# Issuing one tensor's early loads from a second engine's queue in a row-wise Poisson loss

## Chip, cores, metric

One core of one Trainium2 chip. The time is device microseconds of a whole execution; the lower the better. The profile's span (first to last instruction) is 1.34 us shorter than that time, since it leaves out what the device does around the program.

All times below are of fast runs: no kernel's runs differ by more than 0.6%, and the granted clock is 1.0 in every one. Ratios are the mean time of one kernel's fast runs over that of the other's in the same rounds, so they are not quite the ratio of the medians that are quoted.

## The reference

```
log_input, target: 1024 x 4096 float32
loss = exp(log_input) - target * log_input
out  = mean(loss, axis=-1)            # 1024 float32
```

Both inputs are 16.8 MB, the result 4 KB. Per element there is one exponential (ScalarE) and one product with a running sum (VectorE).

## The kernel before

Each of the 128 partitions holds 8 whole rows. Below, "x" is log_input and "t" is target. The loads come in this order: x rows 0-3, t rows 0-3, x rows 4-5, t rows 4-5, x row 6, t row 6, then row 7 in seven small pieces. Rows 0-3 live in x_big and t_big, rows 4-5 in x_mid and t_mid. Row 6 reuses the place of row 0 and row 7 that of row 3, so those loads wait for the work on these rows.

```python
TAIL = [("x", 98), ("t", 50), ("t", 48), ("x", 24), ("t", 18), ("x", 6), ("t", 12)]
# ... cut
    loads = []
    for first, rows in ((0, 4), (4, 2), (6, 1)):
        loads += [("x", first * d, rows * d), ("t", first * d, rows * d)]
# ... cut: TAIL appended, buffers, one semaphore per load
    early = []
    for i, (what, lo, w) in enumerate(loads):
        if what == "x" and lo in (6 * d, 7 * d):
            free = 1 if lo == 6 * d else 4
            nc.sync.wait_ge(exp_done, free)
            nc.sync.wait_ge(prod_done, free)
        src = x_v if what == "x" else t_v
        dma = nc.sync.dma_start(out=place(what, lo, w), in_=src[:, lo : lo + w])
        dma.then_inc(landed[i] if i < len(loads) - 1 else last_ready, 16)
        if lo < 6 * d:
            early.append(dma.ins)
    before_first_barrier(nc, early)     # moves them ahead of the program's first barrier
# ... cut
    # ScalarE, per row: exp with a row sum, waiting for landed[x]; from row 2 on a small
    # "join" ahead of it that adds up row - 2, waiting for that row's product
    # VectorE, per row: product with a row sum, waiting for landed[x] and landed[t]
```

## Time and profile before

| | before |
|---|---|
| median time | 84.02 us (83.93 to 84.27, 3 runs) |
| span in the profile | 82.5 us |
| VectorE, ScalarE busy | 35.6 us, 33.2 us |
| packets on 16 DMA engines | 95.8% of the span, one queue |
| first product on VectorE | 41.12 us |
| first exponential on ScalarE | 21.80 us |

Read the table from the DMA row up. The transfer engines are full; both compute engines are idle for more than half the span, and most of that idle time is at the front, waiting for the first rows. In all lines of the profile DVE is VectorE, ACT is ScalarE and POOL is GpSimd; SPq and ACTq are the queues in which SyncE and ScalarE issue, q1 and q10 the DMA queues that these fill; L129 is a line of the kernel. A packet is one piece of data that an engine moves in one go, here one partition's share of a load. A barrier is a point at which all engines wait for each other; the program has three before the kernel's own work. Where ScalarE waited before the change (the list of waits: engine and line, what it waited for, us in total, times, longest):

```profile
ACT e_dump L155 <- DMA x_big<-in_log_input_dram: 23.6, 3, 17.6
ACT join_dump L141 <- DVE parts L175: 20.3, 6, 16.3
```

ScalarE got rows 0-3 of x early, did two exponentials, and then stood 16.3 us before its first join, until VectorE had a product for it.

### The profile page before, as it was taken

What the parts mean: (1) busy time and instruction counts of PE and PEld (TensorE: products, weight loads), DVE (VectorE), ACT (ScalarE), POOL (GpSimd) and SP (SyncE); (2) the same over time, 40 slices, a digit from 0 to 9 for tenths busy, and PEclk for the clock granted to TensorE, in tenths of its full rate; (3) what the DMA queues carried; (4) which work ended last, traced back from release to release, by engine and by line L of the source; (5) the groups of instructions that cost most, each with busy time, mean ns of one, the idle gap of its engine ahead of it and who ended that gap; (6) DMA issues with size and microseconds to landing.
All of it is one profiled execution on the core that took longest, in us unless ns stands there. A gap on an engine that the chain in (4) does not pass through costs nothing.

```text
span 82.5 us, 131 instructions
## 1 busy us (share of the span) xinstructions
DVE 35.6 (43%) x22; ACT 33.2 (40%) x35; POOL 0.3 (0%) x5
## 2 busy tenths in 40 slices
DVE  0000000000000000000099999999369995993992
ACT  0500000000499920000000998979792496009460
POOL 0000000000000000000000000000000000000000
DMA  9289999929999992999599799799799999999960
GB/s 508 127 381 508 508 508 508 476 95 445 508 508 508 508 413 95 508 508 508 254 508 429 333 508 492 318 460 508 302 453 397 461 421 418 426 402 412 397 231 2
DMA packets 2016, 33.56 MB, mean 407 GB/s; under 512 B 352, under 2 KB 608, under 8 KB 1120
## 3 DMA queue, kind: packets, MB, share of 16 engines
q1 hardware_dynamic: 2016, 33.56, 95.8%
HBM read 33.55 MB, written 0.00 MB: 407 GB/s over the span
## 4 chain that ended last, share of the span: by engine, by line
DMA 72%; DVE 18%; issue 5%; SPq 3%; DVEq 0%
DMA t_big<-in_target_dram 49%; DMA x_big<-in_log_input_dram 23%; DVE t_big L175 17%; SPq L129 3%; DVE t_big L193 1%; DVE parts L175 0%; DVEq L192 0%; SPq L127 0%; DVE all_loss L193 0%
## 5 line engine op out<-in xcount | busy, mean ns | idle before, releaser
L175 DVE CUSTOM_DVE_ANT_0 t_big<-t_big,x_big 128x4096 f32<-128x4096 f32 (+3 forms) x8 | 26.2, 3308 | 43.5 <-DMA t_big<-in_target_dram 43.4
L155 ACT ACTIVATE e_dump<-x_big 128x4096 f32<-128x4096 f32 (+3 forms) x8 | 21.8, 2729 | 23.9 <-DMA x_big<-in_log_input_dram 23.6
L141 ACT ACTIVATE join_dump<-parts 128x2 f32<-128x2 f32 x7 | 1.4, 203 | 20.4 <-DVE parts L175 20.3
L175 DVE CUSTOM_DVE_ANT_0 t_mid<-t_mid,x_mid 128x4096 f32<-128x4096 f32 x2 | 8.8, 4424 | 2.0 <-DMA t_mid<-in_target_dram 2.0
L155 ACT ACTIVATE e_dump<-x_mid 128x4096 f32<-128x4096 f32 x2 | 7.1, 3568 | 0.0
L155 ACT ACT_TABLE_LOAD x1 | 1.3, 1283 | 2.9 <-PEq L48 2.9
L155 ACT ACTIVATION_READ_ACCUMULATOR e_dump<-x_big 128x1 f32 x8 | 1.5, 186 | 0.0
L141 ACT ACTIVATION_READ_ACCUMULATOR join_dump<-parts 128x1 f32 x7 | 1.3, 186 | 0.0
L175 DVE DVE_READ_ACCUMULATOR2_ANT parts<- 128x1 f32 x7 | 0.6, 84 | 0.0
L193 DVE CUSTOM_DVE_ANT_0 t_big<-t_big,x_big 128x390 f32<-128x390 f32 x1 | 0.6, 566 | 0.0
L155 ACT ACTIVATION_READ_ACCUMULATOR e_dump<-x_mid 128x1 f32 x2 | 0.4, 186 | 0.0
L175 DVE DVE_READ_ACCUMULATOR2_ANT t_big<- 128x1 f32 x3 | 0.2, 82 | 0.0
L136 POOL MEMSET x_big<- 128x6 f32 x1 | 0.1, 104 | 2.5 <-POOLq L48 2.5
L227 POOL MEMSET const-uint8-127<- 128x1 uint8 x1 | 0.1, 102 | 0.0
L227 POOL MEMSET const-bfloat16-1.0<- 128x1 bf16 x1 | 0.1, 101 | 0.0
L227 POOL MEMSET const-float32-0.0<- 128x1 f32 x1 | 0.1, 98 | 0.2 <-issue 0.2
L227 POOL MEMSET const-float32-1.0<- 128x1 f32 x1 | 0.1, 98 | 0.0
L193 DVE DVE_READ_ACCUMULATOR2_ANT all_loss<- 128x1 f32 x1 | 0.1, 82 | 0.0
## 6 DMA issues: line engine op xcount, KB each, us to landing
x_mid<-in_log_input_dram SPq DMA_DIRECT2D x1, 4096.0 KB, 49.9
t_mid<-in_target_dram SPq DMA_DIRECT2D x1, 4096.0 KB, 59.2
x_big<-in_log_input_dram SPq DMA_DIRECT2D x1, 2048.0 KB, 19.8
t_big<-in_target_dram SPq DMA_DIRECT2D x1, 2048.0 KB, 24.3
x_big<-in_log_input_dram SPq DMA_DIRECT2D x1, 1568.0 KB, 15.4
t_big<-in_target_dram SPq DMA_DIRECT2D x1, 800.0 KB, 17.0
t_big<-in_target_dram SPq DMA_DIRECT2D x1, 768.0 KB, 18.4
x_big<-in_log_input_dram SPq DMA_DIRECT2D x1, 384.0 KB, 18.9
```

The costliest lines, as they stand in the source:

```text
L129: dma = nc.sync.dma_start(out=place(what, lo, w), in_=src[:, lo : lo + w])
L136: nc.gpsimd.memset(big["x"][:, 4 * d : 4 * d + n_parts], -1.0).then_inc(ones_done, 1)
L141: nc.scalar.activation(out=join_dump[:, 2 * row : 2 * row + 2], in_=parts[:, 2 * row : 2 * row + 2], func=ACT_F.Copy, scale=inv_d, accum_o ...
L155: nc.scalar.activation(out=e_dump[:, col : col + w], in_=place("x", lo, w), func=ACT_F.Exp, bias=0.0, scale=1.0, accum_out=parts[:, 2 * ro ...
L175: nc.vector.tensor_tensor_reduce(out=place("t", lo, w), in0=place("t", lo, w), in1=place("x", lo, w), scale=-1.0, scalar=0.0, op0=ALU.mult ...
L193: nc.vector.tensor_tensor_reduce(out=place("t", lo, w + n_parts), in0=place("t", lo, w + n_parts), in1=place("x", lo, w + n_parts), scale= ...
L227: nc = _bacc.Bacc("TRN2", target_bir_lowering=False, num_devices=1)
```

## The change

All seven loads of t used to stand in SyncE's queue among those of x. The change lets ScalarE issue the two early loads of t (rows 0-3 and 4-5) in its own queue, also ahead of the first barrier, so that x and t set off together and SyncE has two issues less before the barrier.

```diff
-def before_first_barrier(nc, instructions):
+def before_first_barrier(nc, instructions, engine):
 ...
-        if i.engine == mybir.EngineType.SP and i.opcode == "Drain"
+        if i.engine == engine and i.opcode == "Drain"
 ...
-    early = []
+    early = {nc.sync: [], nc.scalar: []}
 ...
-        dma = nc.sync.dma_start(out=place(what, lo, w), in_=src[:, lo : lo + w])
+        issuer = nc.scalar if what == "t" and lo < 6 * d else nc.sync
+        dma = issuer.dma_start(out=place(what, lo, w), in_=src[:, lo : lo + w])
 ...
-            early.append(dma.ins)
-    before_first_barrier(nc, early)
+            early[issuer].append(dma.ins)
+    for issuer, instructions in early.items():
+        before_first_barrier(nc, instructions, issuer.engine)
```

On ScalarE two DMA instructions now stand first; on SyncE two are gone; no other engine's order changes.

## The prediction

> **What bounds the kernel now.** I read the page from the top, then the share of the DMA queue, then windows cut by hand, then the chain and the waits of the two compute engines.
>
> ```profile
> span 82.5 us, 131 instructions
> DVE 35.6 (43%) x22; ACT 33.2 (40%) x35; POOL 0.3 (0%) x5
> ...
> GB/s 508 127 381 508 508 508 508 476 95 445 508 508 508 508 413 95 508 508 508 254 508 429 333 508 492 318 460 508 302 453 397 461 421 418 426 402 412 397 231 2
> ...
> q1 hardware_dynamic: 2016, 33.56, 95.8%
> ```
>
> No compute engine is busy for half the span. The one queue's packets fill 95.8% of 16 DMA engines' 82.5 us, which is 79.0 us. The row of 40 slices seems to disagree: it has slices of 95 and 127 GB/s, which look like holes that a second queue might fill. They are not holes. The packets of the first loads are 64 KB each (a partition's four rows of 16 KB), and at 433 GB/s over 16 engines one takes 65,536 x 16 / 433 GB/s = 2.42 us, more than a slice of 82.5/40 = 2.06 us. A view that books a packet where it starts leaves some slices nearly empty. Windows cut where all engines have just begun a row of packets show this (us of the window, its length, busy us of DVE, ACT and POOL with counts, PE clock, DMA share, GB/s):
>
> ```profile
> 0.00:1.00 1.00, 0.00 (x0) 0.00 (x0) 0.20 (x4) 1.00 0.00 0
> 1.00:20.95 19.95, 0.00 (x0) 1.28 (x1) 0.10 (x1) 1.00 1.01 420
> 20.95:40.28 19.33, 0.00 (x0) 7.42 (x4) 0.00 (x0) 1.00 1.00 434
> 40.28:59.65 19.37, 17.47 (x8) 12.71 (x15) 0.00 (x0) 1.00 1.00 433
> 59.65:80.00 20.35, 17.11 (x11) 11.34 (x15) 0.00 (x0) 1.00 0.99 412
> 80.00:82.50 2.50, 1.04 (x4) 0.43 (x2) 0.00 (x0) 1.00 0.03 2
> ```
>
> The DMA share is 0.99 to 1.01 in every window from 1.0 to 80.0 us. So the span is 1.0 us before the first byte, 79.0 us of all 16 engines working without a break, and 2.5 us after the last byte (last product, result to HBM). The first window's 420 and the last one's 412 GB/s are the fill of the first packets and the small packets of the tail; in the middle the rate is flat at 433 to 434.
>
> The loads arrive in the order of the one queue, as the issue times below plus the page's times to landing say: x rows 0-3 at 21.8, t rows 0-3 at 0.4 + 40.7 = 41.1, x rows 4-5 at 0.9 + 49.9 = 50.8, t rows 4-5 at 1.4 + 59.2 = 60.6, then rows 6 and 7. The timeline shows what SyncE issues first and when VectorE may begin:
>
> ```profile
> 0.00 0.38 SPq L129 DMA_DIRECT2D x_big<-in_log_input_dram  x1
> ...
> 0.43 0.42 SPq L129 DMA_DIRECT2D t_big<-in_target_dram  x1
> 0.89 0.43 SPq L129 DMA_DIRECT2D x_mid<-in_log_input_dram  x1
> 1.37 0.50 SPq L129 DMA_DIRECT2D t_mid<-in_target_dram  x1
> ...
> 21.80 3.59 ACT L155 ACTIVATE e_dump<-x_big 128x4096 f32<-128x4096 f32 x1 [17.58 <-DMA x_big<-in_log_input_dram]
> ...
> 41.12 4.43 DVE L175 CUSTOM_DVE_ANT_0 t_big<-t_big,x_big 128x4096 f32<-128x4096 f32 x1 [41.12 <-DMA t_big<-in_target_dram]
> ...
> 60.55 4.43 DVE L175 CUSTOM_DVE_ANT_0 t_mid<-t_mid,x_mid 128x4096 f32<-128x4096 f32 x1 [1.96 <-DMA t_mid<-in_target_dram]
> ...
> 70.33 4.43 DVE L175 CUSTOM_DVE_ANT_0 t_big<-t_big,x_big 128x4096 f32<-128x4096 f32 x1 [1.00 <-DMA t_big<-in_target_dram]
> ...
> 76.05 1.83 DVE L175 CUSTOM_DVE_ANT_0 t_big<-t_big,x_big 128x1600 f32<-128x1600 f32 x1 [1.28 <-DMA t_big<-in_target_dram]
> ```
>
> After its first row VectorE waits for data three more times: 1.96, 1.00 and 1.28 us. Those 4.2 us are its slack.
>
> **What the Trainium skill says.** "DMA: Bandwidth & Descriptors", section "Issuing engines are not separate DMA queues": DMAs of SyncE and ScalarE run on the same 16 DMA engines, and issuing on several "will only save the time on the sequencer it takes to initiate the DMA". The trace of before, with one queue, cannot show two; what it shows is that four issues took 0.38 to 0.50 us each and all but the first lay under data already moving. The same page, "Where 436 GB/s comes from": the ports carry at most 435.2 GB/s. The trace's 433 to 434 is within half a per cent of it. The same page, "Queues, rings and completion order": each DMA engine goes round robin between queue rows, packet by packet. No run here shows that yet; the prediction rests on it for the order of landing.
>
> **The change part by part.**
>
> Bytes and packets: the same 33.56 MB in the same pieces on the same 16 engines. Nothing removed, nothing added: 0 us.
>
> Issue: t_big moves from second on SyncE (0.43 us) to first on ScalarE, t_mid from fourth (1.37 us) to second there. SyncE is through with its early issues about 0.9 us earlier (two issues of 0.42 and 0.50 us less), so the first barrier opens about that much earlier. What lies behind it is a table load of 1.28 us, after which ScalarE waited 17.6 us for data: 0 us on the path. The first load still leaves SyncE at 0, so the first byte still comes at 1.0 us. With two sequencers generating at once the 16 engines might get their first packet a little more evenly; I allow 0.2 us either way.
>
> Landing: x_big and t_big now share the engines. With equal packets taken in turn both are done when 16.8 MB are through, about 41 us, where t_big landed before. So t_big does not land earlier; x_big lands later, about 38.5 to 41 instead of 21.8. Likewise x_mid and t_mid both at about 59 to 60.5. Row 6 stands in SyncE's queue behind x_mid, and its landing (65.4 and 70.3) follows from bytes alone, as does that of row 7.
>
> VectorE needs both operands, so it starts at 41.1 as before and goes on as before.
>
> ScalarE loses its head start of two exponentials. Alone, an exponential takes 3.81 us from start to start (21.80 to 25.60 in the timeline); with a join in front I take 3.96 (from a join's 45.59 to its exponential's accumulator at 49.30 + 0.19, plus its gap). From 41.1: row 0, row 1 at 44.9, row 2 from 48.7, row 3 from 52.7 to 56.6, wait for x_mid at 60.5 at the latest, rows 4, 5, 6 end at about 64.3, 68.3, 72.3. The first piece of row 7 begins at 74.10 before, when its data land. Slack left: 1.8 us. ScalarE gives up idle time and nothing else.
>
> Buffer gates: row 6's load waits for row 0's exponential and product. The product still ends at 45.5 and the exponential at about 44.9, so the issue stays at 45.6, while SyncE's queue holds x_mid until about 59. Row 7's loads wait for four of each: products at 58.5, exponentials at 56.6, so 58.6 as before, with row 6's data (10 us of it) still ahead. Neither gate starves the engines.
>
> Tail: the loads after row 5 stay on SyncE in the same order and find the other queue empty from about 60 us; 2.5 us after the last byte, as before.
>
> Sum: 0 on bytes, 0 on landing of the later operand, 0 on tail, +-0.2 on the start. 84.02 becomes about 84.0.
>
> **The rivals.**
>
> Faster through bandwidth: two queues keep more reads in flight and lift the rate. For it: the low slices, and 420 GB/s in the first window. Against: the slices are an artefact, and the flat 433 lies at the port's limit. If even the first window ran at 434, its 8.38 MB would take 19.3 instead of 19.95 us: 0.6 us, 83.4, still within 2%.
>
> Slower through unequal shares: if SyncE's queue gets more than its turn, x_mid runs ahead of t_big and VectorE starts late. Its slack is 4.2 us, so t_big may land as late as 45.3 for nothing. For 2% (1.7 us) it must land at 47.0, when 45.4 us x 0.433 = 19.7 MB are through (taking 1.6 us for first byte and fill), of which t_big's 8.39 are 43%: SyncE would need 57% or more. At 60% t_big lands behind all of x_mid, near 50 us, and the time is near 84.0 + 4.7 = 88.7. Equal packet sizes speak against it.
>
> Slower through switching: if alternating between two tensors costs each 64 KB packet 1%, the first 60 us lengthen by 0.6 us: 84.6. Nothing in the trace of before speaks for or against.
>
> **Range and chances.** The centre is 84.0. Runs of before spread from 83.93 to 84.27. A gain of up to 0.5 us at the start and a loss of up to 0.7 from switching or a slightly skewed share give 83.5 to 84.7. Beyond 2% either way (82.3, 85.7) needs a fault in the main argument: above the port's rate I hold 0.01 likely, a share of 57% or more 0.04.
>
> **What would show it.** Right: about 1.00 DMA share from 1.0 to 80 us, now over two queues; ScalarE's first exponential at 38 to 41 us; VectorE's first product at about 41.1; waits of VectorE before rows 4 and 6 still positive; last byte at 80. Wrong: a first product after 45 us, or ScalarE busy without a wait before row 7 (then it has become the bound), or a middle rate away from 433 GB/s.

## The result, and the profile after

84.00 us median (83.94 to 84.18, 6 runs) against 84.02 (83.89 to 84.27, 6 runs): ratio 0.9997, 95% interval 0.9979 to 1.0015. The same.

The page of the changed kernel (span; then queue, packets, MB, share of 16 engines) has two queues whose shares add up to 95.8%, the share that the one queue had:

```profile
span 82.6 us, 131 instructions
...
q1 hardware_dynamic: 1728, 20.98, 60.6%
q10 hardware_dynamic: 288, 12.58, 35.2%
```

The windows of the changed kernel, cut again where a row of packets begins (columns as in the prediction):

```profile
0.00:0.99 0.99, 0.00 (x0) 0.00 (x0) 0.20 (x4) 1.00 0.00 0
0.99:20.90 19.91, 0.00 (x0) 1.28 (x1) 0.10 (x1) 1.00 1.01 421
20.90:40.22 19.32, 0.00 (x0) 0.00 (x0) 0.00 (x0) 1.00 1.00 434
40.22:59.58 19.36, 17.47 (x8) 15.51 (x14) 0.00 (x0) 1.00 1.00 433
59.58:80.01 20.43, 17.07 (x11) 15.94 (x18) 0.00 (x0) 1.00 0.99 411
```

DMA share and rate are those of before in every window: 421, 434, 433, 411 against 420, 434, 433, 412 GB/s. What moved is the ScalarE column: 7.42 us of work in the second window became 0.00, and the two windows after it took it up (15.51 and 15.94 instead of 12.71 and 11.34). The sum of its work is 33.2 us in both kernels.

The timeline of the changed kernel shows the same in single instructions:

```profile
0.00 0.38 SPq L131 DMA_DIRECT2D x_big<-in_log_input_dram  x1
0.12 0.37 ACTq L131 DMA_DIRECT2D t_big<-in_target_dram  x1
...
0.43 0.42 SPq L131 DMA_DIRECT2D x_mid<-in_log_input_dram  x1
0.52 0.45 ACTq L131 DMA_DIRECT2D t_mid<-in_target_dram  x1
...
2.05 1.28 ACT L158 ACT_TABLE_LOAD   x1 [2.05 <-PEq L49]
41.13 3.59 ACT L158 ACTIVATE e_dump<-x_big 128x4096 f32<-128x4096 f32 x1 [37.79 <-DMA x_big<-in_log_input_dram]
41.31 4.42 DVE L178 CUSTOM_DVE_ANT_0 t_big<-t_big,x_big 128x4096 f32<-128x4096 f32 x1 [41.31 <-DMA t_big<-in_target_dram]
...
60.56 3.59 ACT L158 ACTIVATE e_dump<-x_mid 128x4096 f32<-128x4096 f32 x1 [3.56 <-DMA x_mid<-in_log_input_dram]
60.75 4.43 DVE L178 CUSTOM_DVE_ANT_0 t_mid<-t_mid,x_mid 128x4096 f32<-128x4096 f32 x1 [1.97 <-DMA t_mid<-in_target_dram]
...
70.36 4.42 DVE L178 CUSTOM_DVE_ANT_0 t_big<-t_big,x_big 128x4096 f32<-128x4096 f32 x1 [0.83 <-DMA t_big<-in_target_dram]
...
74.14 2.79 ACT L158 ACTIVATE e_dump<-x_big 128x3136 f32<-128x3136 f32 x1 [1.50 <-DMA x_big<-in_log_input_dram]
...
76.07 1.82 DVE L178 CUSTOM_DVE_ANT_0 t_big<-t_big,x_big 128x1600 f32<-128x1600 f32 x1 [1.28 <-DMA t_big<-in_target_dram]
```

The first four lines are the change at work: all early issues are through after about 1 us. The table load begins at 2.05 instead of 2.93 us, which is the earlier barrier, 0.88 us, and then ScalarE stands idle for 37.79 us. Its first exponential starts 19.3 us later than before (41.13 for 21.80), yet before row 7 it still waits 1.50 us for data: it is behind and has caught up. VectorE's lines are those of before, 0.2 us later at the front and 0.02 us at the first piece of row 7.

### The profile page after: what moved, and what is told of

Its sections match the earlier page's. It is cut to its first block, busy times and chain, and to the rows that moved or that the text cites. A ratio compares the mean times of both kernels' runs of the same rounds, so it can differ in the third digit from the quotient of the medians.

```text
span 82.6 us, 131 instructions
## 1 busy us (share of the span) xinstructions
DVE 35.6 (43%) x22; ACT 33.2 (40%) x35; POOL 0.3 (0%) x5
## 4 chain that ended last, share of the span: by engine, by line
DMA 72%; DVE 22%; SPq 3%; issue 1%; DVEq 0%
DMA t_big<-in_target_dram 50%; DMA x_big<-in_log_input_dram 22%; DVE t_big L178 21%; SPq L131 3%; DVE t_big L196 1%; DVEq L195 0%; DVE parts L178 0%; SPq L128 0%; DVE all_loss L196 0%
## 5 line engine op out<-in xcount | busy, mean ns | idle before, releaser
L158 ACT ACTIVATE e_dump<-x_big 128x4096 f32<-128x4096 f32 (+3 forms) x8 | 21.8, 2727 | 41.1 <-DMA x_big<-in_log_input_dram 40.8
```

Source lines behind the costliest of these rows:

```text
L158: nc.scalar.activation(out=e_dump[:, col : col + w], in_=place("x", lo, w), func=ACT_F.Exp, bias=0.0, scale=1.0, accum_out=parts[:, 2 * ro ...
```

## The experiments

The theory: the 16 DMA engines are full, they serve the two queues in turn, piece by piece, and so the time is set by when the *later* operand of each row lands. The change leaves that as it is. The rivals: (a) the second queue brings a gain and a loss that cancel; (b) who issues, and in which order, never matters, only the bytes do; (c) VectorE is on the path as much as the transfers. The first four kernels ran on one chip (kernel before: 83.95 us median of 11 runs there), the last four on another (84.09, 11 runs). All gave correct results.

**e1: ScalarE's loads after the barriers.** The change with its early issue on ScalarE undone; SyncE keeps its own.

```diff
-        if lo < 6 * d:
+        if lo < 6 * d and issuer is nc.sync:
             early[issuer].append(dma.ins)
```

> Theory (the 16 DMA engines are full from 1.0 to 80 us and take packets from the two queues in turn, so who issues and when is hidden): the two target loads now leave ScalarE only after the first barriers, about 1.9 us later than in the changed kernel. The second row of packets starts at 4.0 us in the changed kernel, the new issue lands its first packet near 3 us, so nothing moves: 84.0 us, DMA share 1.00, first product at 41.3. Rival (a gain of the early issue on ScalarE and a loss of alternating cancel each other): without the early issue the loss stands alone, 84.3 us or more.

Measured: 84.08 us (83.91 to 84.12, 6 runs), ratio to before 1.0003 (0.9991 to 1.0016). Rival (a) said 84.3 or more and is out at this size. But one number of mine was wrong: the first product started at 42.55, not 41.3 (timeline).

```profile
1.91 0.37 ACTq L131 DMA_DIRECT2D t_big<-in_target_dram  x1
...
42.55 4.42 DVE L178 CUSTOM_DVE_ANT_0 t_big<-t_big,x_big 128x4096 f32<-128x4096 f32 x1 [42.55 <-DMA t_big<-in_target_dram]
```

By the trace's packet records t's first packet began at 6.5 us, after two of x's and not after one, so x stayed a packet ahead. VectorE took up the 1.2 us out of its waits (1.35 before row 4, 0.40 before row 6, instead of 1.97 and 0.83). So the early issue on ScalarE is worth about 1.2 us in the start of the first product and nothing in the time. Only 0.2 of the 1.2 us is t's last byte (40.92 for 40.73 us); the rest is the notice that tells VectorE of it (last section). Why x got a second packet first is not shown.

**e2: only rows 0-3 of t on ScalarE.** One half of the change.

```diff
-        issuer = nc.scalar if what == "t" and lo < 6 * d else nc.sync
+        issuer = nc.scalar if what == "t" and lo < 4 * d else nc.sync
```

> Only target's rows 0-3 go to ScalarE, rows 4-5 stay behind log_input's on SyncE. Theory: x and t rows 0-3 still share the engines half and half, first product near 41.3; x rows 4-5 land near 50.8 again and t rows 4-5 at 60.5; 84.0 us. Rival (alternating packets costs about 1%): half of the alternation gone, so half of its loss gone, which would show as a small gain over the changed kernel.

Measured: 84.03 us (83.96 to 84.06, 4 runs), ratio 1.0002 (0.9989 to 1.0015). First product at 41.45. As the theory has it, and no sign that alternation costs anything.

**e3: only rows 4-5 of t on ScalarE.** The other half.

```diff
-        issuer = nc.scalar if what == "t" and lo < 6 * d else nc.sync
+        issuer = nc.scalar if what == "t" and 4 * d <= lo < 6 * d else nc.sync
```

> Only target's rows 4-5 go to ScalarE. Theory: they alternate from the start with x rows 0-3, run ahead of t rows 0-3, and t rows 0-3 land only when 21 MB are through: 1.6 + 20.97 / 0.4335 = 50 us. VectorE's slack is about 4.5 us, so the end moves by 50.3 + 7 x 4.35 + 4.35 - 80.5 = 4.6 us: 88.6 us, DMA share still 1.00 up to about 80 us, VectorE without a wait after its first product. Rival (the engine that issues does not matter at all, only bytes do): 84.0 us.

Measured: 88.98 us (88.89 to 89.06, 4 runs), ratio 1.0593 (1.0578 to 1.0607). So half of a neutral change costs 5.9%, and rival (b) is out. The DMA share and the waits of this kernel:

```profile
0.98:80.75 79.77, 29.87 (x13) 31.28 (x29) 0.10 (x1) 1.00 0.99 421
80.75:87.60 6.85, 5.32 (x10) 1.47 (x6) 0.00 (x0) 1.00 0.01 1
...
DVE t_big L178 <- DMA t_big<-in_target_dram: 50.9, 1, 50.9
```

The transfers are as full as ever and over at 80.7 us; but t rows 4-5, wanted last, went in turn with x rows 0-3 and pushed t rows 0-3 back to 50.9. From there VectorE never waited again, so it was the bound, and 6.85 us of the span lie after the last byte instead of 2.5. The expectation was 0.4 us low: I had the last byte of t rows 0-3 at 50.0, the records have 50.46. I had allowed 1.6 us for the first byte and the fill of the first packets; the slowest engine needed 2.1. By the records the first packets start between 1.0 and 1.6 us and take 3.1 us on average instead of 2.42.

**e4: small packets for t.** Rows 0-3 of t as four loads of one row each, all on ScalarE's queue with one semaphore; x keeps its 64 KB packets.

```diff
-        dma = issuer.dma_start(out=place(what, lo, w), in_=src[:, lo : lo + w])
+        piece = d if what == "t" and lo == 0 else w
+        for a in range(lo, lo + w, piece):
+            dma = issuer.dma_start(out=place(what, a, piece), in_=src[:, a : a + piece])
 ... (and VectorE waits for 64 on that semaphore)
```

> Target's rows 0-3 as four loads of one row each on ScalarE (16 KB packets against log_input's 64 KB), one semaphore for all four, waited for at 64. Theory (packet by packet in turn): log_input gets four bytes for each of target's, its rows 0-5 land before target's rows 0-3, which land near 50 us: 88.6 us. Rival (the engines share by bytes, or by issue order): t rows 0-3 still land near 41 us, 84.0 us.

Measured: 89.57 us (89.42 to 89.64, 4 runs), ratio 1.066 (1.0645 to 1.0676). VectorE's wait:

```profile
DVE t_big L180 <- DMA t_big<-in_target_dram: 51.2, 1, 51.2
```

x rows 0-3 were through at 25.7 us and x rows 4-5 at 40.3 (packet records), so x got the share that four bytes to one gives it (two to one for its rows 4-5, whose packets are 32 KB), and t's last byte came at 50.68. The time is 1.0 us over the expectation. Inside the span 0.7 of that can be seen: t's last byte was expected at 50.0, and the last product's start, at 85.1 us by the sum of e3, was at 85.80. The rest is time outside the span: 1.58 us in this kernel's profiled run and 1.59 in the next one's, 1.33 to 1.35 in all the others. These two kernels issue 7 and 10 loads early, the others at most 5; whether that is the cause is not shown.

**e5: small packets for both.** As e4, with `piece = d if lo == 0 else w`, so x is cut too. It tells whether small packets alone explain e4.

> Rows 0-3 of both tensors as four loads of 16 KB packets, on their two queues. Theory: equal packets again, so equal shares, first product near 41.2, 84.0 us; log_input's first exponential starts about 0.6 us (one packet of 16 KB) plus the usual notice after its last byte, not 2.8 us after as in the changed kernel. Rival (more issues or smaller packets cost time in themselves and explain the run with small target packets): slower than 84.5 us.

Measured: 84.46 us (84.37 to 84.48, 4 runs), ratio 1.0043 (1.0026 to 1.0059). So with equal packets the better part of e4's loss is gone: unequal shares made it. What is left is small, and most of it, 0.24 us, is again outside the span. The spans are 82.8 to 82.9 us, those of the kernel before in the same rounds 82.6 to 83.0, about 0.1 us less on average. In the profile the last byte is at 80.34 us, 0.35 later than before, but that profile is of another session, and other runs come near it: 80.23 in e6, on this chip and with one queue, and 80.17 in e1. So a cost of small packets inside the span is at most 0.1 us or so and not shown. My first product was wrong again (42.67, not 41.2), for the reason of e1: x got two packets before t's first. The lag of the notice was right: x's last byte at 39.76, the exponential at 40.84, 1.08 us. The time lies just under the 84.5 us from which I would have given the rival its point; more issues and small packets explain 0.4 of e4's 5.6 us.

**e6: one queue, x row 4 ahead of t rows 0-3.** The kernel before, with its slack on VectorE tried out.

```diff
+    loads[1:4] = [("x", 4 * d, d), ("t", 0, 4 * d), ("x", 5 * d, d), ("t", 4 * d, 2 * d)]
 ...
-        if j == 0 or x_load > t_work[j - 1][2]:
+        if True:
```

The second edit makes VectorE wait for x's load before every product, which the new order needs.

> One queue, log_input's row 4 (2.1 MB, 4.84 us) ahead of target's rows 0-3. Theory: t rows 0-3 land at 41.1 + 4.8 = 45.96, VectorE runs without a wait through seven rows to 45.96 + 7 x 4.347 = 76.4, where the last row's data came at 76.05 before: the slack is used up and 0.2 to 0.4 us over, 84.2 to 84.4 us. Rival (VectorE was on the path all along): the whole 4.8 us, 88.8 us.

Measured: 84.13 us (84.09 to 84.26, 6 runs), ratio 1.0005 (0.9990 to 1.0020). Rival (c) is out: VectorE started 5.1 us later and nearly nothing came of it. The timeline:

```profile
46.22 4.43 DVE L176 CUSTOM_DVE_ANT_0 t_big<-t_big,x_big 128x4096 f32<-128x4096 f32 x1 [46.22 <-DMA t_big<-in_target_dram]
...
76.65 1.82 DVE L176 CUSTOM_DVE_ANT_0 t_big<-t_big,x_big 128x1600 f32<-128x1600 f32 x1
```

The second line has no wait in brackets any more: the data were there, and VectorE came to them at 76.65 instead of 76.05. In the profile the last product starts 0.37 us later than before (80.87 for 80.50), of the size expected; the median moved by 0.04 us, which the runs do not tell from nothing. So the slack is 5.10 - 0.37 = 4.7 us.

**e7 and e8: no load ahead of the barriers**, in the changed kernel (e7) and in the kernel before (e8). In e7 `if lo < 6 * d:` becomes `if False:`; in e8 the same, and the call of before_first_barrier goes.

> The changed kernel with no load ahead of the barriers, on either queue. Theory: the first byte is on the path, and it comes about 1.2 us later (slowest engine at the first barrier about 0.5 us, three barriers about 0.7 us): about 85.2 us. Rival (issue is hidden also for the first load): 84.0 us.

> The kernel before with no load ahead of the barriers. Theory: as the run with two queues and none early, 85.2 us, within 0.3% of it, since the second load's issue is hidden here too. Rival (a second issuing engine pays where the issue is late): this one slower by 0.4 us or more than its two-queue sister.

Measured: e7 85.46 us (85.30 to 85.54, 4 runs), ratio 1.0161 (1.0142 to 1.0180); e8 85.43 us (85.19 to 85.46, 4 runs), ratio 1.0154 (1.0135 to 1.0174). The windows of e7:

```profile
1.00:2.30 1.30, 0.00 (x0) 0.01 (x1) 0.10 (x1) 1.00 0.00 0
2.30:81.50 79.20, 34.58 (x19) 32.74 (x34) 0.00 (x0) 1.00 1.00 424
```

The first packet starts at 2.37 us in both, 1.37 later than in the kernels with early loads, and the times are 1.37 and 1.34 us longer. The first byte is on the path one for one. The delay was expected at 1.2 us: the sum had 0.7 us for the barriers, and they took some 0.9 if the slowest engine was ready at about 0.5 us as assumed, since the first issue starts at 1.38. A second issuing engine buys nothing here either, where its issues are later: the two differ by 0.03 us.

## Why the prediction was right

**What bounds it.** Shown. The 16 engines work from 1.0 to 80.0 us in both kernels, and moving the first byte (e7, e8) moves the end by the same amount.

**Issue and barrier.** Shown. The barrier opens 0.88 us earlier (0.9 predicted) and ScalarE's wait grows instead. The start moved by less than the 0.2 us allowed: the first packet begins at 1.008 us before and 0.998 after. One reading in the prediction is wrong: not "all but the first" of the four issues lay under data already moving. The first byte moved at 1.0 us; the second issue (0.43 to 0.85) was over by then, and of the four only the last lay wholly behind it. They were off the path all the same, since each engine had its first 64 KB packet of x to move, until 4.0 us or later, before it could use them.

**Landing.** Right in the result and shown by the packet records: x and t go strictly in turn, one piece each per engine. t_big's last byte is at 40.73 us in the changed kernel, 40.75 before. Where the prediction was loose is x_big: "about 38.5 to 41". Its last byte was at 38.32, but ScalarE could only start at 41.13, since the notice of completion comes a turn later (last section). This put the first exponential at 41.13, just outside the 38 to 41 that the prediction named as a sign of being right. The prediction had no term for this delay. It cost nothing, because ScalarE had slack; where it struck VectorE instead, by about 1 us in e1, that had slack too.

**VectorE and ScalarE.** The four rows of ScalarE predicted at 41.1, 44.9, 48.7 and 52.7 us started at 41.13 and 44.93, with the joins ahead of the next two at 48.73 and 52.72; the slack before row 7 is 1.50 us instead of 1.8, because the sum left out the join ahead of it (72.34 to 72.64 us). VectorE's slack was put at 4.2 us and is 4.7 (e6): the brackets leave out some 0.1 us of read-out that overlaps the next product, and a short wait late in the tail. The term was too small and on the safe side.

**The rivals.** Bandwidth: the middle rate is 434 and 433 GB/s as before, no gain. Unequal shares: it did not happen, but what it would do is real. e3 and e4 made t rows 0-3 land late by two routes, behind t rows 4-5 in e3 and behind x rows 4-5 in e4, which are as many bytes. The predicted 88.7 us for t behind all of x rows 4-5 stands beside 88.98 and 89.57. No run made the queues take unequal turns. Switching: no run shows a cost; the mean 64 KB packet after the first row takes 2,418 to 2,419 ns with one queue and with two. (The 0.6 us of that rival counted the 32 KB packets in as well; the 64 KB ones alone, up to 41 us, would give 0.4.)

Left open: 0.24 us outside the span in the two kernels with more early loads. VectorE's start lagged its load's last byte by 0.58 us with two queues and 0.37 with one; the traces show where this comes from. The notices of x and t rows 0-3 leave within 0.01 us of each other (40.73 and 40.74 us for the last engine), yet the two engines waiting start 0.18 us apart, ScalarE at 41.13 and VectorE at 41.31. The same 0.17 to 0.19 us lies between them after rows 4-5 (60.56 and 60.75), in e2 (41.27 and 41.45) and twice in e7. Why the second notice takes longer is open.

## What to carry to other kernels

When all DMA engines are full, as here, a second issuing queue changes only the order in which bytes arrive; ask which operand lands last, and whether the change moves that. Two queues share in turn by piece, so the sizes of the pieces and what stands in each queue decide who goes first: put the loads that are wanted together in step, and do not send a late one ahead on the second queue (e3, +5.9%). A slice of low GB/s in a profile whose packets are longer than the slice is no hole; cut windows at packet boundaries before believing it.

## What the Trainium skill lacked or had wrong

- "DMA: Bandwidth & Descriptors", "Queues, rings and completion order", has each engine take turns between queues packet by packet, a packet being typically some 9 to 17 descriptors. Turns packet by packet are what the runs show, but a turn was one contiguous piece of 64, 32 or 16 KB of a partition in all of them. No page says what follows: shares go by the size of the pieces. With 64 KB against 16 KB, x rows 0-3 were through at 25.7 us instead of 38.3 (e4).
- The same section says that the notice of completion lands only after every earlier write of its engine, in whichever queue. It does not say that the notice takes a turn of its own, nor what that costs: with two busy queues a load can be reported one piece of the *other* queue late. In e1 the turn can be seen: x's notice is written from 37.92 us on, then t has another 64 KB, and the next data in x's queue start only at 40.34. From the packet records, last byte of the load to the start of the engine that waited for it:

```
kernel, load               last byte   reader starts   lag    piece of the other queue between
before, x rows 0-3           21.43        21.80        0.37   none (one queue)
before, t rows 0-3           40.75        41.12        0.37   none (one queue)
e4,     x rows 0-3           25.73        26.73        1.00   16 KB (0.61 us)
e1,     t rows 0-3           40.92        42.55        1.63   32 KB (1.21 us)
after,  x rows 4-5           58.89        60.56        1.67   32 KB (1.21 us)
after,  x rows 0-3           38.32        41.13        2.81   64 KB (2.42 us)
e1,     x rows 0-3           36.09        38.91        2.82   64 KB (2.42 us)
```

  The lag is 0.37 to 0.46 us plus the time of that piece. Where the other queue has only a notice to write in between, as for t rows 0-3 in the changed kernel, the lag is 0.58. In the changed kernel the records of the 4-byte completion writes of x rows 0-3 lie at 40.22 to 40.73 us, after t's last piece and not after x's own.
- "DMA: Bandwidth & Descriptors", "Latency and other measured facts", gives about 600 ns to the first byte for loads issued by SyncE or ScalarE, and does not say from when it counts. Here 1.0 us passed from the start of the first issue to the start of its first packet (0.998 us), and 0.98 us in e7 (issue at 1.38, packet at 2.37). From the end of the issuing instruction, which took 0.38 and 0.36 us, it was 0.62 us in both, which agrees with the page.
